# Two transformer blocks on one core: own PSUM tiles for the last two chunks of a product, the first two chunks side by side, the last residual first, the lambdas early

## The chip, the core and the metric

The kernel runs on one core of a Trainium2 chip. The core has TensorE for matrix products, VectorE and ScalarE for work on tiles, GpSimd (POOL) for small work, and SyncE (SP), whose queue issues nearly all transfers. They run side by side, each through its own list of instructions in order, and wait for one another by semaphores. The metric is the time of one execution in device microseconds.

## What is computed

Everything is float32, 256 positions of 1024 features, batch 1. The first block, once:

```python
proj = rmsnorm(h, g) @ w_in                    # q, k, v, u, y
attn = dilated_mixture_attention(rope(q), rope(k), v)
rec  = bidirectional_rglru(conv(u), ...) * gelu(y)
h = h + concat([attn, rec]) @ w_out
h = h + memory_cross_attention(rmsnorm(h), rmsnorm(mem), w_cq, w_ck, w_cv, w_co)
h = h + square(relu(rmsnorm(h) @ w_mlp_in)) @ w_mlp_out      # 1024 -> 4096 -> 1024
x = rmsnorm(h)
```

and the second, twice (two layers):

```python
z = rmsnorm(x) @ w_in_2                        # inputs of four mixers and 4 x 1024 gates
merged = sum(sigmoid(gate[n]) * (mixer[n](z) @ w_branch[n]) for n in range(4))
x = x + merged @ w_out_2                       # mixers: latent attention, Fourier, differential
h2 = rmsnorm(x)                                #   attention (with a lambda), gated recurrence
x = x + (silu(h2 @ w_gate) * (h2 @ w_up)) @ w_down           # 1024 -> 2 x 2816 -> 1024
```

The lambda of the differential attention is `exp(sum(lq1*lk1)) - exp(sum(lq2*lk2))` and a constant; the recurrence has lower bounds for its forget gates. Both come from small parameters alone.

## The kernel before

Features lie on the 128 partitions, positions along the rows, so the 1024 features are eight slices `k` of 128. A product is computed in **chunks** of 128 output features; a chunk needs all K slices of its input (K = 8, for `w_mlp_out` 32, for `w_down` 22).

**Weights.** All weights come as one stream of blocks, 128 x 1024 elements of 512 KB each, `w`, in the order in which `plan` lists them: kind "F" goes through all K slices of one chunk before the next, kind "T" through all listed columns of one slice before the next slice. Five blocks are in flight at most. ScalarE rounds a block to the type fp32r, `whi` (L353), VectorE computes the remainder `wlo` (L354), and inputs are treated alike: `xx`, `hd`, `fw` have a high and a low part. `lin` multiplies hi by hi, hi by lo and lo by hi, three matmuls of 256 columns (L378 to L380, in `mm3`). `lin_w` does the same with two: L575 takes high and low part of the input side by side, 512 columns, L576 adds the low weights, 256 columns.

**PSUM and consumers.** `lin` puts a pair of chunks into one tile `pl` of 2 KB a partition. `lin_w` puts a pair into one tile `pw` of 4 KB, each chunk in its own half; there are two such tiles. What is done with a finished pair (`consume`) is noted in `self.pend` and emitted by `flush` after the next pair's first chunks. With `fine=True` the last two chunks are not taken as a pair: each is consumed as soon as it is there.

**The seam.** The consumer of the products that end in the residual stream is `residual` (L1126 to L1138). For `lin_w`, ScalarE copies one part to `rs` (L588), VectorE adds the other (L589), multiplies by the norm's factor (L1133) and adds to `h` (L1134). Then `prep` makes the slice `xx` of the next product's input: its high part on ScalarE (L385), its low part on VectorE (L389), and squares for the next norm. So each product's first chunk needs, with its last slice `k` = 7, the residual of the last chunk of the product before.

**Order.** The program is written stage by stage; a scheduler then orders the instructions of each engine by its own estimates of time and by priorities (`high_priority(n)` moves work ahead by n). So an engine may do work of the next stage between two chunks of this one. `mixers` run beside the products by such priorities.

**Small parameters.** `hgrn_bounds` (L1235) makes the bounds of the forget gates; `diff_lambdas` (L1253) loads `lq`, multiplies (`lqp`, L1262), sums (`lqs`), exponentiates on GpSimd (`lqe`). Both are called at the start of the second block (L1779, L1780). The tables of a layer (`tabs`, `dt`, L1291 to L1303) and its small weights (`sw`, L1282) are loaded before each layer. At the start of the kernel, SyncE also loads `mem` (L747) and swaps halves of `qe` for the rotary embedding through `sw<-qe` (L698).

Of the kernel before, what the change touches and what calls it, by code (L numbers as in the profile page):

```python
# [9 lines left out]
F32 = mybir.dt.float32  # L10
# [9 lines left out]
T = 256  # L20
D = 1024
KD = D // 128
# [6 lines left out]
NW = 5  # L29
SB = 8  # L30
WARM = 36
G4, H2 = 16, 12
A0, A1 = 2, 4
X0, X1 = 1, 3
D0, D1 = 2, 4
M0, M1 = 1, 2
HA, HR, HM, HN = 200, 100, 100, 400

# [28 lines left out]
def plan():  # L67

    p = []
    r = np.arange  # L70

    def f(key, idx, cols):
        p.append((key, idx, cols, "F"))

    def t(key, idx, cols):
        p.append((key, idx, cols, "T"))

    t("w_in", (0,), 1536 + r(512))
    f("w_in", (0,), r(512))
    f("w_in", (0,), 512 + r(512))  # L80
    t("w_in", (0,), 1024 + r(512))
    f("w_in", (0,), 2048 + r(512))
    f("w_ck", (0,), r(512))
    f("w_out", (0,), r(1024))
    f("w_cq", (0,), r(512))
    t("w_cv", (0,), r(512))
    f("w_co", (0,), r(1024))
    f("w_mlp_in", (0,), r(4096))
    f("w_mlp_out", (0,), r(1024))
    for l in range(LAYERS):  # L90
        f("w_in_2", (l,), _forget_cols())
        t("w_in_2", (l,), _cols("fnet"))
        for n in ("hq", "hg", "dq", "dk", "c_kv"):
            f("w_in_2", (l,), _cols(n))
        f("w_in_2", (l,), _krope_cols())
        f("w_in_2", (l,), _cols("c_q"))
        t("w_in_2", (l,), np.concatenate([_cols("hi"), _cols("dv")]))
        for n in BRANCHES:
            w = 1024 if n != BRANCHES[-1] else 256
            for o in range(0, 1024, w):  # L100
                f("w_in_2", (l,), _cols("gate")[n * 1024 + o:n * 1024 + o + w])
                f("w_branch_2", (l, n), o + r(w))
        f("w_out_2", (l,), r(1024))
        f("w_gate_up_2", (l,), np.concatenate(
            [np.concatenate([j * 128 + r(128), FF2 + j * 128 + r(128)]) for j in range(FF2 // 128)]))
        f("w_down_2", (l,), r(1024))
    return p
# [372 lines left out]
def run(gen):  # L480
    for _ in gen:
        pass
# [26 lines left out]
class Body(Kern):  # L509
# [24 lines left out]
        for f, a in p:  # L534
            f(*a)

    def lin(self, key, idx, M, act, consume, K=KD, fine=False, half=False, m0=0):


        self.segment(key, idx, M * 128, "F")  # L540
        for m in range(0, M, 2):
            n = min(2, M - m)
            ps = self.psl("pl").rearrange("p (c t) -> p c t", c=2)
            one = fine and m + 2 >= M
            for c in range(n):
                for k in range(K):
                    wh, wl = self.wtile()
                    xh, xl = act(k)
                    self.mm3(ps[:, c, :], wh, wl, xh, xl, k == 0, k == K - 1)
                self.tick()  # L550
                if c == n - 1 or one:
                    self.flush()
                if one:
                    consume(m0 + m + c, ps[:, c:c + 1], 1)
                if half and c < n - 1:
                    yield
            if n == 1:
                self.tick()
            if not one:
                self.pend.append((consume, (m0 + m, ps[:, :n], n)))  # L560
            yield

    def lin_w(self, key, idx, M, act, consume, K=KD, fine=False):


        self.segment(key, idx, M * 128, "F")
        mm = self.nc.tensor.matmul
        for m in range(0, M, 2):
            ps = self.pw.tile([128, 2, 2, T], F32, name="pw", tag="pw")
            one = fine and m + 2 >= M  # L570
            for c in range(2):
                for k in range(K):
                    wh, wl = self.wtile()
                    x = act(k)
                    mm(ps[:, c], wh, x, start=k == 0, stop=False, skip_group_check=True)  # L575
                    mm(ps[:, c, 0], wl, x[:, 0], start=False, stop=k == K - 1, skip_group_check=True)  # L576
                self.tick()
                if c == 1 or one:
                    self.flush()
                if one:  # L580
                    consume(m + c, ps[:, c:c + 1], 1)
            if not one:
                self.pend.append((consume, (m, ps, 2)))
            yield
# [300 lines left out]
    def act(self, xh, xl):  # L885
        return lambda k: (xh[:, k], xl[:, k])
# [24 lines left out]
    def block1(self):  # L911
# [235 lines left out]
        def c_cq(k, ps, n):  # L1147
            V.tensor_tensor(cq[:, k:k + n], ps, self.bT(r2["b"], n), op=OP.mult)

        run(self.lin("w_cq", (0,), 4, xact, c_cq))  # L1150
        ch, cl = self.g4("ch", F32R), self.g4("cl", F32R)

        def cross():
# [25 lines left out]
        self.flush()  # L1179
        r3 = self.norm_later(n3, "n3")  # L1180


        hid = [self.g4(f"hd{i}", F32R, [128, 2, 2, T]) for i in range(16)]

# [6 lines left out]
        run(self.lin_w("w_mlp_in", (0,), 32, lambda k: self.xx[:, k], c_mlp))  # L1191
        self.flush()
        b3 = r3["b"]
        V.tensor_tensor(b3, b3, b3, op=OP.mult)
# [80 lines left out]
    def layer(self, l, rx, nxt):  # L1275
# [385 lines left out]
        def c_merge(n, m):  # L1661
# [4 lines left out]
            def f(k, ps, c):  # L1666
# [7 lines left out]
                if n == BRANCHES[-1]:  # L1674
# [4 lines left out]
        items = [self.lin(k2, L, 4, x, c_forget), self.lin_t(k2, L, 256, x, c_fx), ("start", mixers[1]), self.lin(k2, L, 2, x, c_hq), ("start", mixers[3]),  # L1679
                 self.lin(k2, L, 2, x, c_hg), self.lin(k2, L, 2, x, scaled(dqe)), self.lin(k2, L, 2, x, scaled(dke)),  # L1680
                 ("start", mixers[2]),
                 self.lin(k2, L, 1, x, c_kv), self.lin(k2, L, 1, x, c_kr), self.lin(k2, L, 3, x, scaled(cq)),
# [2 lines left out]
        for n in BRANCHES:  # L1685
# [4 lines left out]
            for m in range(0, 8, M):  # L1690
# [7 lines left out]
        self.flush()  # L1698
        n6 = Norm(self)
        run(self.lin("w_out_2", L, 8, lambda k: (mh[k // 4][:, k % 4], ml[k // 4][:, k % 4]),  # L1700
                     self.residual(n6, self.G(f"ln_ffn{l}")), fine=True))
        self.flush()
        r6 = self.norm_later(n6, "n6")

# [8 lines left out]
            f = fw[k // 4][:, k // 2 % 2]  # L1713
            self.split(f[:, 0], f[:, 1], t[:, 1])

        run(self.lin_w("w_gate_up_2", L, 44, lambda k: self.xx[:, k], c_glu))
# [89 lines left out]
```

## Time and profile before

| | |
|---|---|
| median of 3 runs | 1310.23 us |
| lowest, highest | 1309.72, 2054.62 us |
| the profiled execution | 1312.75 us, of which its span is 1311.0 |
| mean granted clock of TensorE | 0.986 |
| busy: TensorE, its weight loads | 1269.3 us (97%), 1153.5 us (88%) |
| busy: VectorE, ScalarE, GpSimd | 919.6 us (70%), 721.9 us (55%), 85.0 us (6%) |
| read from memory | 208.37 MB, 160 GB/s over the span |

The span runs from the first to the last instruction. Busy time of an engine is the time in which it worked on instructions; matmuls overlap, and one that follows another starts before the other's end. In a timeline the number in square brackets is the idle time of the engine just before the instruction, and the arrow names what ended it. The granted clock is a share of TensorE's full speed: 1.00 is 2.4 GHz, 0.50 is 1.2 GHz.

### The profile page before, as it was taken

How to read it: one execution, taken by the hardware profiler on the slowest of the kernel's cores; microseconds unless marked ns; L12 is line 12 of the kernel's file. 1: busy time of each engine (PE TensorE's matmuls, PEld its weight loads, DVE VectorE, ACT ScalarE, POOL GpSimd, SP SyncE). 2: the span in 40 equal slices, each digit the busy share in tenths (PEclk: the TensorE clock that was granted, in tenths of full speed). 3: DMA queues.
4: the chain of work that ended last, by engine and by line, in shares of the span. 5: the costliest groups of instructions: out<-in, count | busy, mean ns of one | idle time of the engine just before them, and what ended most of it. 6: DMA issues, size and time to landing. Idle time of an engine off the chain costs nothing.

```text
span 1311.0 us, 21638 instructions
## 1 busy us (share of the span) xinstructions
PE 1269.3 (97%) x8514; PEld 1153.5 (88%) x8514; DVE 919.6 (70%) x1396; ACT 721.9 (55%) x1132; POOL 85.0 (6%) x105
## 2 busy tenths in 40 slices
PE   8989989999989999999999999999999999999998
PEld 8876978888879998899988887899989899888887
DVE  5986648775557985667767775669866677777754
ACT  5777556554446456544555553464574545655542
POOL 8010000000001300100000000003001000000000
PEclk9889999999999999999999999999998999999999
DMA  7642435555564452245555565554522355555562
GB/s 262 202 130 79 147 110 193 189 188 187 191 209 156 157 181 81 97 147 188 179 179 193 187 206 208 167 165 147 191 96 85 126 177 179 184 188 190 191 190 68
DMA packets 68741, 216.07 MB, mean 165 GB/s; under 512 B 10392, under 2 KB 16280, under 8 KB 68640
## 3 DMA queue, kind: packets, MB, share of 16 engines
q1 hardware_dynamic: 68592, 214.66, 50.1%
q8 instruction: 67, 1.10, 0.3%
q14 instruction: 34, 0.28, 0.1%
q0 software_dynamic: 48, 0.03, 0.0%
HBM read 208.37 MB, written 1.05 MB: 160 GB/s over the span
## 4 chain that ended last, share of the span: by engine, by line
PE 85%; DVE 5%; ACT 4%; POOL 2%; issue 2%; DMA 2%; SPq 0%; DVEq 0%; ACTq 0%; POOLq 0%
PE pw L575 27%; PE pw L576 14%; PE pl L379 11%; PE pl L378 11%; PE pl L380 11%; PE ph L1388 2%; DVE wlo L354 2%; ACT whi L353 1%; PE pl L620 1%; PE pl L619 1%; PE pl L621 1%; POOL rt L808 1%; ACT p L669 1%; PE pq L1541 1%; PE pod L1491 1%
## 5 line engine op out<-in xcount | busy, mean ns | idle before, releaser
L353 ACT ACTIVATE whi<-w 128x1024 fp32r<-128x1024 f32 (+1 forms) x386 | 403.9, 1050 | 463.3 <-issue 154.9
L354 DVE TENSOR_TENSOR wlo<-w,whi 128x1024 fp32r<-128x1024 f32 (+1 forms) x386 | 467.2, 1212 | 251.6 <-ACT whi L353 250.5
L575 PE MATMUL pw<-xx,whi 128*128 128x512 f32 x960 | 334.3, 392 | 0.3 <-DVE xx L389 0.3
L576 PE MATMUL pw<-xx,wlo 128*128 128x256 f32 x960 | 269.5, 281 | 0.1
L378 PE MATMUL pl<-xx,whi 128*128 128x256 f32 x912 | 262.0, 288 | 7.7 <-ACT xx L385 4.0
L380 PE MATMUL pl<-xx,wlo 128*128 128x256 f32 x912 | 263.8, 290 | 3.5 <-DVE wlo L354 3.5
L379 PE MATMUL pl<-xx,whi 128*128 128x256 f32 x912 | 262.4, 288 | 0.0
L575 PEld LDWEIGHTS pw<-xx,whi 128*128 128x128 f32 x960 | 179.7, 187 | 40.2 <-DVE xx L389 1.0
L378 PEld LDWEIGHTS pl<-xx,whi 128*128 128x128 f32 x912 | 176.8, 194 | 10.2 <-ACT xx L385 4.4
L380 PEld LDWEIGHTS pl<-xx,wlo 128*128 128x128 f32 x912 | 176.8, 194 | 7.4 <-DVE wlo L354 4.3
L576 PEld LDWEIGHTS pw<-xx,wlo 128*128 128x128 f32 x960 | 181.4, 189 | 0.4 <-DVE wlo L354 0.4
L379 PEld LDWEIGHTS pl<-xx,whi 128*128 128x128 f32 x912 | 176.8, 194 | 0.6 <-DVE xx L389 0.2
L575 PE MATMUL pw<-fw,whi 128*128 128x512 f32 x352 | 125.9, 401 | 2.6 <-DVE fw L387 1.7
L576 PE MATMUL pw<-fw,wlo 128*128 128x256 f32 x352 | 99.7, 283 | 0.8 <-DVE wlo L354 0.8
L575 PE MATMUL pw<-hd,whi 128*128 128x512 f32 x256 | 90.4, 397 | 2.7 <-DVE rs L589 2.7
L575 PEld LDWEIGHTS pw<-fw,whi 128*128 128x128 f32 x352 | 66.9, 190 | 19.4 <-DVE fw L387 2.0
L576 PE MATMUL pw<-hd,wlo 128*128 128x256 f32 x256 | 72.2, 282 | 0.0
L576 PEld LDWEIGHTS pw<-fw,wlo 128*128 128x128 f32 x352 | 67.3, 191 | 1.4 <-DVE wlo L354 1.4
L575 PEld LDWEIGHTS pw<-hd,whi 128*128 128x128 f32 x256 | 48.6, 190 | 13.8 <-DVE rs L589 3.0
L576 PEld LDWEIGHTS pw<-hd,wlo 128*128 128x128 f32 x256 | 49.1, 192 | 0.0
L378 PE MATMUL pl<-oh,whi 128*128 128x256 f32 x128 | 36.8, 291 | 0.7 <-ACT oh L385 0.7
L379 PE MATMUL pl<-ol,whi 128*128 128x256 f32 x128 | 36.6, 287 | 0.6 <-DVE ol L387 0.6
(429 smaller groups left out, 1997.3 us busy)
## 6 DMA issues: line engine op xcount, KB each, us to landing
w<-in_W_dram SPq DMA_DIRECT2D x378, 512.0 KB, 3.4
w<-in_W_dram SPq DMA_DIRECT2D x8, 256.0 KB, 4.7
sw<-in_S_dram SPq DMA_DIRECT2D x4, 512.0 KB, 6.2
h<-in_xT_dram SPq DMA_DIRECT2D x8, 128.0 KB, 4.8
mem<-in_memT_dram SPq DMA_DIRECT2D x2, 512.0 KB, 5.5
sw<-qe SPq DMA_DIRECT2D x16, 64.0 KB, 3.5
dt<-in_C_dram SPq DMA_DIRECT2D x4, 256.0 KB, 7.5
dqs<-dhi SPq DMA_DIRECT2D x16, 64.0 KB, 3.8
```

What stands on the lines that cost most here:

```text
L353: self.nc.scalar.activation(hi, w, AF.Copy)
L354: self.nc.vector.tensor_tensor(lo, w, hi.bitcast(F32), op=OP.subtract)
L378: mm(out, wh, xh, start=first, stop=False, skip_group_check=shared)
L379: mm(out, wh, xl, start=False, stop=False, skip_group_check=shared)
L380: mm(out, wl, xh, start=False, stop=last, skip_group_check=shared)
L575: mm(ps[:, c], wh, x, start=k == 0, stop=False, skip_group_check=True)
L576: mm(ps[:, c, 0], wl, x[:, 0], start=False, stop=k == K - 1, skip_group_check=True)
L619: mm(o, xh[:, s], wh, start=(k == 0), stop=False)
L620: mm(o, xh[:, s], wl, start=False, stop=False)
L621: mm(o, xl[:, s], wh, start=False, stop=(k == K - 1))
L669: nc.scalar.activation(p[:, q], src[:, q], AF.Exp, bias=nm[:, q:q + 1], scale=scale if number else scale[:, q:q + 1], accum_out=den[:, q:q ...
L1388: nc.tensor.matmul(ps[:, k], hk[:, 2 * hp + k // 2, s], qz[:, 2 * hp + k // 2, s], start=True, stop=True)
```

## The change

1. With `fine=True`, each of the last two chunks gets a PSUM tile of its own, in `lin` and in `lin_w`.
2. With the new `side=True`, the first two chunks of a product are computed side by side over the slices: slice 0 for both, slice 1 for both, and so on. Their weights come in that order in the stream (kind "T" for the first 256 columns). It is set for `w_cq`, `w_mlp_in`, the forget columns that begin `w_in_2`, `w_out_2` and `w_gate_up_2`.
3. The consumers of the last two chunks are emitted at high priority (`HF` = 400).
4. `hgrn_bounds` and `diff_lambdas` are called before `w_mlp_in` and no longer at the start of the second block.
5. In `lin`, with `half=True`, noted consumers are also flushed after the first chunk of a pair.
6. The buffers of the tag `h2` are 10 instead of 12.

```diff
-G4, H2 = 16, 12
+G4, H2 = 16, 10
...
-HA, HR, HM, HN = 200, 100, 100, 400
+HA, HR, HM, HN, HF = 200, 100, 100, 400, 400
...
+    def tf(key, idx, cols):
+        t(key, idx, cols[:256])
+        f(key, idx, cols[256:])
...
-    f("w_cq", (0,), r(512))
+    tf("w_cq", (0,), r(512))
...
-    f("w_mlp_in", (0,), r(4096))
+    tf("w_mlp_in", (0,), r(4096))
...
-        f("w_in_2", (l,), _forget_cols())
+        tf("w_in_2", (l,), _forget_cols())
...
-        f("w_out_2", (l,), r(1024))
-        f("w_gate_up_2", (l,), np.concatenate(
+        tf("w_out_2", (l,), r(1024))
+        tf("w_gate_up_2", (l,), np.concatenate(
...
+    def order(self, key, idx, M, K, m, side):
+        if m == 0:
+            if side:
+                self.segment(key, idx, 256, "T")
+            else:
+                self.segment(key, idx, M * 128, "F")
+        elif m == 2 and side:
+            self.segment(key, idx, (M - 2) * 128, "F")
+        n = min(2, M - m)
+        if side and m == 0:
+            return [(c, k) for k in range(K) for c in range(n)]
+        return [(c, k) for c in range(n) for k in range(K)]
...
     # in lin
-            ps = self.psl("pl").rearrange("p (c t) -> p c t", c=2)
             one = fine and m + 2 >= M
-            for c in range(n):
-                for k in range(K):
-                    wh, wl = self.wtile()
-                    xh, xl = act(k)
-                    self.mm3(ps[:, c, :], wh, wl, xh, xl, k == 0, k == K - 1)
+            ps = [self.psl("pl").rearrange("p (c t) -> p c t", c=2) for _ in range(n if one else 1)]
+            for i, (c, k) in enumerate(self.order(key, idx, M, K, m, side)):
+                o = ps[c][:, 0] if one else ps[0][:, c]
+                wh, wl = self.wtile()
+                xh, xl = act(k)
+                both = side and m == 0
+                self.mm3(o, wh, wl, xh, xl, k == 0 and not (both and c), k == K - 1, both)
+                if (i + 1) % K:
+                    continue
+                c = i // K
                 self.tick()
-                if c == n - 1 or one:
+                if c == n - 1 or one or half:
                     self.flush()
                 if one:
-                    consume(m0 + m + c, ps[:, c:c + 1], 1)
+                    with self.tc.high_priority(HF):
+                        consume(m0 + m + c, ps[c][:, :1], 1)
...
     # in lin_w
             ps = self.pw.tile([128, 2, 2, T], F32, name="pw", tag="pw")
-            one = fine and m + 2 >= M
-            for c in range(2):
-                for k in range(K):
-                    wh, wl = self.wtile()
-                    x = act(k)
-                    mm(ps[:, c], wh, x, start=k == 0, stop=False, skip_group_check=True)
-                    mm(ps[:, c, 0], wl, x[:, 0], start=False, stop=k == K - 1, skip_group_check=True)
+            po = [ps[:, 0], ps[:, 1]]
+            if one:
+                po[1] = self.pw.tile([128, 2, 2, T], F32, name="pw", tag="pw")[:, 0]
+            for i, (c, k) in enumerate(self.order(key, idx, M, K, m, side)):
+                wh, wl = self.wtile()
+                x = act(k)
+                mm(po[c], wh, x, start=k == 0, stop=False, skip_group_check=True)
+                mm(po[c][:, 0], wl, x[:, 0], start=False, stop=k == K - 1, skip_group_check=True)
...
                 if one:
-                    consume(m + c, ps[:, c:c + 1], 1)
+                    with self.tc.high_priority(HF):
+                        consume(m + c, po[c].rearrange("p (o a) t -> p o a t", o=1), 1)
...
         r3 = self.norm_later(n3, "n3")
+        self.hgrn_bounds()
+        self.diff_lambdas()
...
         rx = self.between(n4, n5)
-        self.hgrn_bounds()
-        self.diff_lambdas()
```

**TensorE at the end of `w_mlp_out`**, from the seventh to the eighth output chunk (`pw` is the tile in PSUM with its number, `hd0` to `hd15` the hidden slices, two in each). Before:

```order
L575 MATMUL pw_3660<-hd15_2251,whi_3685 128x512
L576 MATMUL pw_3660<-hd15_2251,wlo_3686 128x256
L575 MATMUL pw_3660<-hd0_2236,whi_3707 128x512
L576 MATMUL pw_3660<-hd0_2236,wlo_3708 128x256
L575 MATMUL pw_3660<-hd0_2236,whi_3707 128x512
```

With the change:

```order
L601 MATMUL pw_3685<-hd15_2276,whi_3711 128x512
L602 MATMUL pw_3685<-hd15_2276,wlo_3712 128x256
L601 MATMUL pw_3686<-hd0_2261,whi_3733 128x512
L602 MATMUL pw_3686<-hd0_2261,wlo_3734 128x256
L601 MATMUL pw_3686<-hd0_2261,whi_3733 128x512
```

Before, the eighth chunk goes into the tile of the seventh, 3660; now it goes into another one, 3686.

**VectorE at the end of `w_mlp_out`**, from the next layer's tables to the last slice of the next product's input (`rs` and `h` with 256 columns are the residual of the last chunk). Before:

```order
L1302 TENSOR_SCALAR dt<-dt,pt 128x256 x2
L354 TENSOR_TENSOR wlo<-w,whi 128x1024
L1303 TENSOR_SCALAR dt<-dt,pt 128x256 x2
L354 TENSOR_TENSOR wlo<-w,whi 128x1024 x2
L589 TENSOR_TENSOR rs<-pw,rs 128x256
L1133 TENSOR_TENSOR rs<-rs,n3b 128x256
L1262 TENSOR_TENSOR lqp<-lq 128x64 x2
L1134 TENSOR_TENSOR h<-h,rs 128x256
L1264 TENSOR_REDUCE lqs<-lqp 128x4
L1305 TENSOR_SCALAR gc<-pt 128x1
L1306 TENSOR_SCALAR gc<-pt 128x1
L389 SCALAR_TENSOR_TENSOR xx<-h,misc,xx 128x256
```

With the change:

```order
L1332 TENSOR_SCALAR tabs<-tabs,pt 128x256 x2
L1333 TENSOR_SCALAR tabs<-tabs,pt 128x256
L358 TENSOR_TENSOR wlo<-w,whi 128x1024
L1335 TENSOR_SCALAR dt<-dt,pt 128x256 x2
L1336 TENSOR_SCALAR dt<-dt,pt 128x256 x2
L358 TENSOR_TENSOR wlo<-w,whi 128x1024
L619 TENSOR_TENSOR rs<-pw,rs 128x256
L1163 TENSOR_TENSOR rs<-rs,n3b 128x256
L1164 TENSOR_TENSOR h<-h,rs 128x256
L358 TENSOR_TENSOR wlo<-w,whi 128x1024
L393 SCALAR_TENSOR_TENSOR xx<-h,misc,xx 128x256
```

`lqp`, `lqs` and `gc` have left this place, and a `wlo` now stands between `h` and `xx`; the tables and some `wlo` stand ahead of `rs`, as they did. Behind the last chunk TensorE now has 58 matmuls of the next product ahead of the first that needs the last `xx`, where it had 42.

**SyncE near the start of the kernel**, from the weight blocks that follow the first tables to the first rope swap (`gb` are gate matrices). Before:

```order
L339 DMA w<-in_W_dram 128x1024 x4
L747 DMA mem_519<-in_memT_dram 128x1024
L747 DMA mem_520<-in_memT_dram 128x1024
L339 DMA w<-in_W_dram 128x1024
L741 DMA gb_462<-in_gw_dram 64x8x64 x2
L741 DMA gb_463<-in_gw_dram 64x8x64
L339 DMA w<-in_W_dram 128x1024
L741 DMA gb_463<-in_gw_dram 64x8x64
L339 DMA w<-in_W_dram 128x1024 x3
L698 DMA sw<-qe 32x512 x8
```

With the change:

```order
L343 DMA w<-in_W_dram 128x1024 x5
L771 DMA gb_462<-in_gw_dram 64x8x64 x2
L771 DMA gb_463<-in_gw_dram 64x8x64 x2
L343 DMA w<-in_W_dram 128x1024 x3
L777 DMA mem_521<-in_memT_dram 128x1024
L777 DMA mem_522<-in_memT_dram 128x1024
L343 DMA w<-in_W_dram 128x1024
L728 DMA sw<-qe 32x512 x4
L343 DMA w<-in_W_dram 128x1024
```

The two transfers of `mem` stood behind four weight blocks and ahead of the gate matrices; now they stand behind eight blocks and the gate matrices, one weight block ahead of the first `sw<-qe`.

## Rows read from the trace of the kernel before

**Rows 1.** The page's first part: busy time, share of the span, instructions.

```profile
PE 1269.3 (97%) x8514; PEld 1153.5 (88%) x8514; DVE 919.6 (70%) x1396; ACT 721.9 (55%) x1132; POOL 85.0 (6%) x105
```

**Rows 2.** Waits of TensorE: us in total, times, longest.

```profile
PE pl L378 <- ACT xx L385: 4.0, 2, 2.7
PE pw L575 <- DVE rs L589: 3.6, 2, 2.7
```

**Rows 3.** TensorE's timeline: start, us, line, operation [idle before, releaser].

```profile
81.31 0.47 PE L415 MATMUL mbp<-ct,mr 128*128 128x128 f32 x1 [3.53 <-POOL mr L397]
...
371.21 0.79 PE L575 MATMUL pw<-hd,whi 128*128 128x512 f32 x1 [2.67 <-DVE rs L589]
...
388.68 0.28 PE L379 MATMUL pl<-xx,whi 128*128 128x256 f32 x1
388.80 0.28 PE L380 MATMUL pl<-xx,wlo 128*128 128x256 f32 x1
391.79 0.80 PE L378 MATMUL pl<-xx,whi 128*128 128x256 f32 x2 [2.70 <-ACT xx L385]
...
637.63 0.39 PE L379 MATMUL pl<-mgl,whi 128*128 128x256 f32 x1 [0.22 <-DVE mgl L389]
...
661.46 0.50 PE L575 MATMUL pw<-xx,whi 128*128 128x512 f32 x1 [0.15 <-DVE xx L389]
...
838.55 0.39 PE L378 MATMUL pl<-xx,whi 128*128 128x256 f32 x1 [0.38 <-ACT whi L353]
...
839.81 0.39 PE L380 MATMUL pl<-xx,wlo 128*128 128x256 f32 x1 [0.76 <-DVE wlo L354]
...
853.90 0.51 PE L378 MATMUL pl<-xx,whi 128*128 128x256 f32 x2 [1.25 <-ACT xx L385]
...
1298.44 0.50 PE L575 MATMUL pw<-fw,whi 128*128 128x512 f32 x1 [0.93 <-DVE rs L589]
```

**Rows 4.** TensorE by stretch: us, busy (matmuls), granted clock, DMA share, GB/s.

```profile
81.30:84.30 3.00, 2.99 (x12) 0.50 0.33 104
...
371.20:374.40 3.20, 3.19 (x10) 0.50 0.59 188
375.00:378.20 3.20, 3.20 (x20) 1.00 0.91 295
...
391.80:394.90 3.10, 3.10 (x14) 0.50 0.00 0
```

**Rows 5.** VectorE's timeline, columns as in Rows 3.

```profile
51.74 0.68 DVE L964 TENSOR_TENSOR sw<-sw,rope 128x512 f32<-128x512 f32 x1
...
205.28 0.47 DVE L389 SCALAR_TENSOR_TENSOR xx<-h,pt,xx 128x256 fp32r<-128x256 f32 x1
...
370.74 0.42 DVE L589 TENSOR_TENSOR rs<-pw,rs 128x256 f32<-128x256 f32 x1
...
380.64 0.61 DVE L1299 TENSOR_SCALAR tabs<-tabs,pt 128x256 f32<-128x256 f32 x2 [2.62 <-DMA tabs<-in_C_dram]
...
390.49 0.36 DVE L1262 TENSOR_TENSOR lqp<-lq 128x64 f32<-128x64 f32 x2 [3.35 <-DMA lq<-in_lq_dram]
390.77 0.42 DVE L1134 TENSOR_TENSOR h<-h,rs 128x256 f32<-128x256 f32 x1
...
391.76 0.48 DVE L389 SCALAR_TENSOR_TENSOR xx<-h,misc,xx 128x256 fp32r<-128x256 f32 x1 [0.26 <-ACT xx L385]
```

**Rows 6.** The page's costliest groups, the split on VectorE: busy, mean ns, idle before.

```profile
L354 DVE TENSOR_TENSOR wlo<-w,whi 128x1024 fp32r<-128x1024 f32 (+1 forms) x386 | 467.2, 1212 | 251.6 <-ACT whi L353 250.5
```

**Rows 7.** SyncE's timeline, columns as in Rows 3.

```profile
40.16 1.87 SPq L698 DMA_DIRECT2D sw<-qe  x3
...
200.40 0.33 SPq L339 DMA_DIRECT2D w<-in_W_dram  x1
```

**Rows 8.** The page's DMA issues: times, KB each, us to landing.

```profile
mem<-in_memT_dram SPq DMA_DIRECT2D x2, 512.0 KB, 5.5
```

**Rows 9.** The tile `qe`, sixteen swap transfers: us from issue to landing.

```profile
DMA to landing us min/median/max: 1.9/3.5/6.2
```

More of the change, by code (lines that the diff above doesn't have):

```diff
@@ L535, in flush, with lin @@
             f(*a)
-    def lin(self, key, idx, M, act, consume, K=KD, fine=False, half=False, m0=0):
-        self.segment(key, idx, M * 128, "F")
+    def order(self, key, idx, M, K, m, side):
[10 more added lines that the diff above has]
+        return [(c, k) for c in range(n) for k in range(K)]
+    def lin(self, key, idx, M, act, consume, K=KD, fine=False, half=False, m0=0, side=False):
         for m in range(0, M, 2):
             n = min(2, M - m)
-            ps = self.psl("pl").rearrange("p (c t) -> p c t", c=2)
             one = fine and m + 2 >= M
-            for c in range(n):
-                for k in range(K):
-                    wh, wl = self.wtile()
-                    xh, xl = act(k)
-                    self.mm3(ps[:, c, :], wh, wl, xh, xl, k == 0, k == K - 1)
+            ps = [self.psl("pl").rearrange("p (c t) -> p c t", c=2) for _ in range(n if one else 1)]
[8 more added lines that the diff above has]
+                c = i // K
                 self.tick()
-                if c == n - 1 or one:
+                if c == n - 1 or one or half:
                     self.flush()
                 if one:
-                    consume(m0 + m + c, ps[:, c:c + 1], 1)
+                    with self.tc.high_priority(HF):
+                        consume(m0 + m + c, ps[c][:, :1], 1)
                 if half and c < n - 1:
@@ L559, in lin, with lin_w @@
             if not one:
-                self.pend.append((consume, (m0 + m, ps[:, :n], n)))
+                self.pend.append((consume, (m0 + m, ps[0][:, :n], n)))
             yield
-    def lin_w(self, key, idx, M, act, consume, K=KD, fine=False):
-        self.segment(key, idx, M * 128, "F")
+    def lin_w(self, key, idx, M, act, consume, K=KD, fine=False, side=False):
         mm = self.nc.tensor.matmul
         for m in range(0, M, 2):
+            one = fine and m + 2 >= M
             ps = self.pw.tile([128, 2, 2, T], F32, name="pw", tag="pw")
-            one = fine and m + 2 >= M
-            for c in range(2):
-                for k in range(K):
-                    wh, wl = self.wtile()
-                    x = act(k)
-                    mm(ps[:, c], wh, x, start=k == 0, stop=False, skip_group_check=True)
-                    mm(ps[:, c, 0], wl, x[:, 0], start=False, stop=k == K - 1, skip_group_check=True)
+            po = [ps[:, 0], ps[:, 1]]
[6 more added lines that the diff above has]
+                mm(po[c][:, 0], wl, x[:, 0], start=False, stop=k == K - 1, skip_group_check=True)
+                if (i + 1) % K:
+                    continue
+                c = i // K
                 self.tick()
@@ L1148, in c_cq @@
             V.tensor_tensor(cq[:, k:k + n], ps, self.bT(r2["b"], n), op=OP.mult)
-        run(self.lin("w_cq", (0,), 4, xact, c_cq))
+        run(self.lin("w_cq", (0,), 4, xact, c_cq, side=True))
         ch, cl = self.g4("ch", F32R), self.g4("cl", F32R)
@@ L1189, in c_mlp @@
             self.split(hid[k // 2][:, :, 0], hid[k // 2][:, :, 1], t2)
-        run(self.lin_w("w_mlp_in", (0,), 32, lambda k: self.xx[:, k], c_mlp))
+        run(self.lin_w("w_mlp_in", (0,), 32, lambda k: self.xx[:, k], c_mlp, side=True))
         self.flush()
@@ L1678, in layer @@
         mixers = {n: urgent(self.tc, m, HM) for n, m in ((3, hgrn()), (2, diff()), (0, mla()), (1, fnet()))}
-        items = [self.lin(k2, L, 4, x, c_forget), self.lin_t(k2, L, 256, x, c_fx), ("start", mixers[1]), self.lin(k2, L, 2, x, c_hq), ("start", mixers[3]),
+        items = [self.lin(k2, L, 4, x, c_forget, side=True), self.lin_t(k2, L, 256, x, c_fx), ("start", mixers[1]), self.lin(k2, L, 2, x, c_hq), ("start", mixers[3]),
                  self.lin(k2, L, 2, x, c_hg), self.lin(k2, L, 2, x, scaled(dqe)), self.lin(k2, L, 2, x, scaled(dke)),
@@ L1700, in layer @@
         run(self.lin("w_out_2", L, 8, lambda k: (mh[k // 4][:, k % 4], ml[k // 4][:, k % 4]),
-                     self.residual(n6, self.G(f"ln_ffn{l}")), fine=True))
+                     self.residual(n6, self.G(f"ln_ffn{l}")), fine=True, side=True))
         self.flush()
@@ L1714, in c_glu @@
             self.split(f[:, 0], f[:, 1], t[:, 1])
-        run(self.lin_w("w_gate_up_2", L, 44, lambda k: self.xx[:, k], c_glu))
+        run(self.lin_w("w_gate_up_2", L, 44, lambda k: self.xx[:, k], c_glu, side=True))
         self.flush()
```

## The prediction

> **What bounds the kernel now.** The page's first part comes first: TensorE is busy 97% of the span [rows 1], so the kernel can only become faster by fewer matmuls (the change has as many) or by closing the places in which TensorE stands. Idle is only 1311.0 - 1269.3, about 42 us. The view of TensorE's waits says for whom it stands: 4.0 us for ScalarE's `xx`, 3.6 us for VectorE's `rs` [rows 2]. TensorE's timeline then places each wait [rows 3]. The 3.6 us for `rs` are two waits before the last output chunk of a product: 2.67 at 371.21 (`w_mlp_out`) and 0.93 at 1298.44 (the second `w_down`). The 4.0 us for `xx` are the first matmul that reads the last eighth of the next stage's input: 2.70 at 391.79 and 1.25 at 853.90. So the stage to look at is the seam: a product's last chunks, the residual sum, the preparation of `xx`, the next product's first chunks.
>
> The windows on TensorE give the hidden part of the price. After each of the two long waits the granted clock is 0.50, the level of 1.2 GHz: 3.20 us at 371.20 with 10 matmuls where 20 fit at 375.00, and 3.10 us at 391.80 again at 0.50 [rows 4]. Half the work of about 3.2 us is lost, 1.6 us each. I count such a stretch behind waits of this length alone, not behind the 0.93 and 1.25.
>
> **Part A, own tile.** In `lin_w` both chunks of a pair share one tile, so the last chunk's first matmul waits until the `rs` of the chunk before has read it. VectorE took up that `rs` at 370.74 [rows 5] and TensorE went on at 371.21 [rows 3]. After the change it writes a tile of its own, whose former user is the pair before. That pair was due a whole chunk earlier, 64 matmuls at 20 in 3.20 us [rows 4] or some 10 us, so the estimate for the wait is zero. What is removed: 2.67 + 1.6 of half clock at 371, and 0.93 at 1298: 5.2 us. What could eat it: TensorE now wants the next split weights 2.7 us sooner. At 375.00 it takes them at full speed and without a gap [rows 4], so I take nothing. The rule that speaks against this part is the Trainium skill's, "PSUM — Partial Sum Buffer", section "PSUM bank collisions raise a hardware error": engines are to be kept apart by bank, so a reader in another bank stops no matmul. The two halves of the tile are two banks; by that rule there would be no wait to remove, and the sum would be 5.2 us smaller. The rows show the wait, with VectorE's `rs` as its releaser, so here the program's dependency goes by the tile, and the trace decides.
>
> **Part B, the lambdas early.** At the end of `w_mlp_out`, VectorE finished its part of `rs` at 387.1 (390.49 - 3.35) and then stood 3.35 us in `lqp` for a small transfer of `lq`. `h` came behind it at 390.77 and the last `xx` at 391.76 [rows 5]. TensorE had run through the 42 matmuls that didn't need it and waited 2.70 us [rows 3]. With `lqp` gone, `h` starts at 387.1 and `xx` 1.0 us later, before the cover runs out. At 0.12 us from matmul to matmul (388.68, 388.80 [rows 3]) 42 last 5.0 us, and the change raises them to 58, 7.0 us. A `wlo` of 1.2 us [rows 6] now stands between `h` and `xx`; 58 matmuls carry that too. Removed: 2.70 + 1.6 = 4.3 us.
>
> `lqp` is not gone but moved: it stands now before the last `xx` of the seam from `w_co` to `w_mlp_in`, which came at 205.28 [rows 5]. By SyncE's order its transfer goes out right behind the weight block that went out at 200.40 [rows 7]; if it takes 5.5 us as the transfers of `mem` did [rows 8], it lands at about 206, near the time at which `xx` was due. Bounds: nothing, and a hold as long as the one seen, 3.35 [rows 5]. Since landing and need nearly meet, and TensorE's cover there grows by some 0.8 us, I expect a wait between 0 and 0.9 and take 0.4. The rest of the lambdas, and the bounds of the forget gates, are some ten short VectorE operations beside the cross-attention's tail, where TensorE already waits in places: 0 to 0.7, I take 0.3.
>
> **Part C, side by side and the last residual first.** At the first layer's `w_down`, 18 matmuls of the next layer were slipped in before the last chunk. They waited 0.38 and 0.76 for their weights, and left only 24 behind the last chunk, 2.9 us, so that `xx` was 1.25 late [rows 3]. The change puts none ahead and 58 behind (7.0 us); `xx` needed 2.9 + 1.25 = 4.2. Removed: 0.38 + 0.76 + 1.25 = 2.4 us. Side by side also doubles the matmuls per eighth of the input wherever a stage starts: the waits of 0.22 at 637.63 (for `mgl`) and 0.15 at 661.46 (for `xx`) [rows 3] have a twin each in the second layer, at 1100.64 and 1124.47; 0.74 us in all. The interleaving itself adds no matmul and no weight load. The order of the weights in the stream changes, not their number or size; the pool of residual buffers shrinks from 12 to 10, and by the order at most about 7 are in use. I cost both at nothing.
>
> **The start.** The order of SyncE's queue shows a move that the diff doesn't: the two 512 KB transfers of `mem` now go out after eight weight blocks and the gate tables, and ahead of the rope swap's transfers. A transfer of `mem` takes 5.5 us to land [rows 8]. The swap's first transfers were issued from 40.16 to 42.0 [rows 7] and took at most 6.2 us [rows 9], so they were there by 48.2; VectorE first reads a swapped tile at 51.74 [rows 5], a slack of 3.5 us at least. With `mem` ahead I estimate that they land about 4 us later, so this comes out about even: 0, with bounds of 7 us gained (the GpSimd wait of 3.53 at 81.31 [rows 3] and the stretch at half clock behind it [rows 4], some 3 us, if the order around it becomes kinder) and 5 us lost.
>
> **Sum.** 5.2 + 4.3 + 2.4 + 0.7 = 12.6; less 0.4 and 0.3: about 12 us. The profiled execution took 1312.75 us (1311.0 of span and 1.75 around it), 2.5 above the median of the runs shown, 1310.23. In its terms the result is 1300.7, as a median **1298**.
>
> **The rivals.** *The gains are eaten again.* The last residual is put first, but in the order of VectorE the tables of the next layer (`tabs`, `dt`) and two `wlo` still stand ahead of it. `tabs` came at 380.64, held by its transfer [rows 5], 9.4 us after the last chunk's first matmul. Behind it stand seven table operations of 0.3 us each and two `wlo` of 1.2 [rows 5, 6], 4.5 us. In all that is 14 us, against about 11 for the chunk at full clock (64 matmuls); with the gate opening about a microsecond earlier at full clock, `rs` starts 2 to 3 us behind the chunk. Then come twice `rs` and `h`, 0.4 each, the `wlo` and `xx`, 3.3: 5.3 to 6.3 of the 7.0 that the cover lasts. If the transfer lands 1 to 2 us later than this, TensorE waits again and B's half-clock stretch comes back: up to 4.3; with 0.9 more for `lqp` and its own stretch, 6.8. Then 5 to 8 us are left: 1302 to 1306, and up to 1309 if a third seam is hit. For it: the margin is thin. Against it: the transfer is released by the last chunk's first matmuls, which now run at full clock, so it should be earlier.
>
> *The start gains too.* The order around 81 us has `mbp` 22 rows later on TensorE, which gives GpSimd's `mr` more time. If its 3.53 and the slow stretch of 3 go as well: 1298 - 6.5 = 1291, and with a little less idle before it, 1287 to 1291.
>
> *Slower than before.* VectorE stands at the first multiplication with a swapped tile, because `mem` lies ahead of it in the queue; `wlo` stands behind it, so TensorE runs dry and its clock falls to 1.2 GHz, as it did after the waits of 2.7 and 3.5 us [rows 3, 4]. Slack is about 4 us. For a loss beyond the 12 us won, the hold must be about 9 us (9 idle and some 3 of half clock), that is, the tile must land later than about 61. Two landings of `mem`, 5.5 us each and one after the other, put it at 48 + 11 = 59 only if nothing overlaps, which I hold unlikely. It would give 1313 to 1322.
>
> *The change doesn't do what it says*: the scheduler orders the work by its own estimates and gives each seam back. The order speaks against it: own tile, the place of `lqp` and the 58 matmuls are all there. About 1307 to 1311.
>
> **How the numbers follow.** Forecast (1292 to 1302): 0.58. Gains eaten (1302 to 1309): 0.22. The start gains too (1287 to 1292): 0.12. Slower (1313 to 1322): 0.05. No effect: 0.03. The range reaches from the lower end of the start's gain to the upper end of the eaten gains: 1288 to 1309, which leaves out the slower case, most of no effect and the rims. Two per cent, 26 us, is about what a measurement of this kernel can tell from no change. Faster than 1284 needs every case's gain at once and more: 0.03. Slower than 1336 needs a hold at the start twice as long as the slower rival's: 0.02. Within: 0.95.
>
> **What the changed profile would show.** A: no wait for `rs` before the last chunk of `w_mlp_out` and of the second `w_down`, and full clock there. B: no `lq` among VectorE's waits at the seam to the next block, and `xx` before its 58 matmuls end. C: no wait for `whi`, `wlo` or `xx` around the first `w_down`. Wrong: a wait of over 1 us for `xx` behind `tabs`, a hold in `lqp` near 205, or a wait for `sw` on VectorE near 52. If the stalls are gone and the time is not, something else than TensorE's idle time was lost, and its busy time or clock must show it.

## The result, and the profile after

The changed kernel took 1289.35 us (median of 4 runs, 1287.15 to 1292.48), the kernel before 1309.97; the ratio is 0.984, with a 95% interval of 0.982 to 0.986. That is 20.6 us less, where 12 were predicted: inside the stated range (1288 to 1309), beyond the band of the forecast (1292 to 1302), and in that of the rival by which the start gains too (1287 to 1292). One run of the kernel before took 2054.62 us; the ratio leaves it out.

The page's first part, of the changed kernel:

```profile
span 1285.3 us, 21650 instructions
...
PE 1257.4 (98%) x8514; PEld 1146.8 (89%) x8514; DVE 918.1 (71%) x1396; ACT 720.3 (56%) x1132; POOL 85.2 (7%) x105
```

Its view of TensorE's waits, us in total, times and longest:

```profile
PE po L1118 <- ACT pts L720: 3.2, 3, 1.7
PE pl L382 <- ACT whi L357: 2.9, 2, 2.5
PE pl L384 <- DVE wlo L358: 2.1, 1, 2.1
PE sd L1506 <- ACT p L699: 1.6, 2, 1.1
```

The two rows that led before, the waits for `xx` and for `rs` [rows 2], are gone. What leads now lies in the attention, whose row for `pts` was 1.5 us in 2 waits before, and at 32 to 34 us, where both kernels wait. In the windows of [rows 4], the clock is full:

```profile
81.30:84.30 3.00, 3.00 (x28) 1.00 0.37 128
371.20:374.40 3.20, 3.20 (x26) 1.00 1.04 403
391.80:394.90 3.10, 3.10 (x28) 1.00 0.00 0
```

These windows hold other work than before, since the stages come earlier (the last chunk of `w_mlp_out` starts at 361.37), but the mean granted clock is 1.00 over the whole stretch from 40 to 511 us. The same TensorE work needs less busy time too (1257.4 against 1269.3 us [rows 1]), mostly because a matmul at half clock counts as busy for twice as long [rows 4]: up to the last matmul this trace has 13.7 us at half clock, that of before 34.1. Not all of that is the change: two more traces of the changed kernel (experiment 4) have 23.9 and 27.3.

The last residual of `w_mlp_out`, on VectorE (the row of work that [rows 5] shows from `tabs` to `xx`):

```profile
370.19 0.62 DVE L1332 TENSOR_SCALAR tabs<-tabs,pt 128x256 f32<-128x256 f32 x2 [0.82 <-DMA tabs<-in_C_dram]
...
374.83 0.42 DVE L619 TENSOR_TENSOR rs<-pw,rs 128x256 f32<-128x256 f32 x1
375.29 0.43 DVE L1163 TENSOR_TENSOR rs<-rs,n3b 128x256 f32<-128x256 f32 x1
375.75 0.42 DVE L1164 TENSOR_TENSOR h<-h,rs 128x256 f32<-128x256 f32 x1
376.50 1.23 DVE L358 TENSOR_TENSOR wlo<-w,whi 128x1024 fp32r<-128x1024 f32 x1 [0.33 <-ACT whi L357]
377.65 0.48 DVE L393 SCALAR_TENSOR_TENSOR xx<-h,misc,xx 128x256 fp32r<-128x256 f32 x1
```

The chunk's last matmul started at 372.35; `rs` came 2.5 us behind it and `xx` ended at 378.13, 5.8 behind it. The 58 matmuls last 7.0. TensorE didn't stand there.

**Where the time went.** From the traces: the time from the last matmul of one product to the last of the next, in us. The first stage ends at `mbp`.

| up to the last matmul of | before | after | after, second trace | own tile alone | without own tile |
|---|---|---|---|---|---|
| (`mbp`) | 81.31 | 79.66 | 80.56 | 82.07 | 79.83 |
| `w_out` | 72.39 | 65.99 | 65.99 | 68.66 | 69.93 |
| `w_co` | 48.62 | 49.72 | 49.73 | 49.01 | 47.33 |
| `w_mlp_in` | 88.30 | 88.23 | 88.22 | 89.40 | 87.68 |
| `w_mlp_out` | 93.17 | 88.75 | 88.75 | 88.75 | 94.64 |
| `w_out_2`, first layer | 274.66 | 267.78 | 269.38 | 270.47 | 270.63 |
| `w_gate_up_2` | 121.04 | 122.96 | 122.96 | 124.92 | 120.18 |
| `w_down_2` | 70.00 | 63.40 | 64.74 | 64.06 | 67.38 |
| `w_out_2`, second layer | 271.97 | 268.24 | 269.95 | 269.92 | 269.70 |
| `w_gate_up_2` | 120.86 | 122.95 | 122.96 | 124.92 | 122.22 |
| `w_down_2` | 63.74 | 62.68 | 62.68 | 61.78 | 63.99 |
| sum to the last matmul | 1306.06 | 1280.37 | 1285.91 | 1293.95 | 1293.53 |

A gate stage that grows by 2 us only takes work that the stage ahead of it gave up (matmuls that were slipped in before), so the two are read together. Four places carry the gain: the first two stages together 8.1 us; `w_mlp_out` 4.4; the first layer's `w_out_2` with its gate stage 5.0 (3.4 in the second trace), where the wait at 391 stood; and the first `w_down_2` 6.6 (5.3). Of the last, some 2.2 us are only work that moved to the next stage (18 matmuls of 0.12), and 1.7 are a stretch at half clock behind a wait for `fw`, which no term of the prediction names and which none of the three traces of the changed kernel has. The two traces of one and the same program differ by 5.5 us, so the pair of profiles (25.7 apart) flatters the change; the comparison of runs is the measure.

### The profile page after: what moved, and what is told of

It reads as the page before. It is cut to its first block, busy times and chain, and to the rows that moved or that the text cites. A ratio compares the mean times of both kernels' runs of the same rounds, so it can differ in the third digit from the quotient of the medians.

```text
span 1285.3 us, 21650 instructions
## 1 busy us (share of the span) xinstructions
PE 1257.4 (98%) x8514; PEld 1146.8 (89%) x8514; DVE 918.1 (71%) x1396; ACT 720.3 (56%) x1132; POOL 85.2 (7%) x105
## 4 chain that ended last, share of the span: by engine, by line
PE 89%; DVE 3%; ACT 2%; POOL 2%; DMA 1%; issue 1%; SPq 1%; DVEq 0%; ACTq 0%; POOLq 0%
PE pw L601 28%; PE pw L602 14%; PE pl L383 11%; PE pl L382 11%; PE pl L384 11%; PE ph L1421 2%; PE pl L649 1%; PE pl L650 1%; PE pl L651 1%; POOL rt L838 1%; PE ptp L717 1%; PE pq L1574 1%; ACT p L699 1%; SPq L1488 1%; PE pod L1524 1%
```

## The experiments

All were run against the kernel before on the same chip, and the ratios are to it. The first four do one part alone, or nothing.

**1. The own tile alone.** The hunks of the diff on `ps` and `po`, without side by side, priority and the rest:

```diff
+            po = [ps[:, 0], ps[:, 1]]
+            if one:
+                po[1] = self.pw.tile([128, 2, 2, T], F32, name="pw", tag="pw")[:, 0]
...
-                    mm(ps[:, c], wh, x, start=k == 0, stop=False, skip_group_check=True)
+                    mm(po[c], wh, x, start=k == 0, stop=False, skip_group_check=True)
```

> The kernel before with one part of the change: an own PSUM tile for each of the last two chunks. Theory (the wait is by the tile): no wait of TensorE for rs before the last chunk of w_mlp_out and of the second w_down, and no half clock at 371; that is 2.67 + 1.6 + 0.93 = 5.2 us. By the order of TensorE this part alone also ends the 18 matmuls that were slipped in before the last chunk of the first w_down, so some of the 2.4 us of that seam go too: 5 to 7.5 us in all, about 1303 to 1305 where the kernel before takes 1310. The hold in lqp at the end of w_mlp_out stays, with its 2.70 and its half clock. Rival (the last chunk waits for VectorE anyway, by the weights or by rs itself): the wait moves behind the last chunk and the time is that of before within 1.5 us.

Measured: 1298.38 us, ratio 0.991 (0.990 to 0.993), some 11 us. Both waits for `rs` are gone, and so are all three waits at the first `w_down_2`. The hold in `lqp` stayed, with this on TensorE:

```profile
385.55 0.38 PE L379 MATMUL pl<-xx,whi 128*128 128x256 f32 x1 [2.12 <-DVE xx L389]
```

On VectorE `lqp` stands behind `h` in this kernel, and the last `xx` waited for it all the same. The own tile is more than half of the gain, more than I expected of it: the rows of Part A and of Part C at the first `w_down_2` make 7.6 us (5.2 and 2.4), and no experiment says where the other 3 come from.

**2. The lambdas early, alone.**

```diff
+        self.hgrn_bounds()
+        self.diff_lambdas()
...
         rx = self.between(n4, n5)
-        self.hgrn_bounds()
-        self.diff_lambdas()
```

> The kernel before with the calls of the bounds and lambdas put ahead of w_mlp_in, nothing else. Theory: the 2.70 us for xx at 391.79 and the half clock behind it go, 4.3 us, and the new place costs at most 0.9: 1306 to 1307. Rival 1 (the hold in lqp only moves): a wait of VectorE for lq of 1 us or more near 205, TensorE waits there, about 1309 to 1310. Rival 2 (the last xx is late for another reason, tabs or rs): TensorE still waits over 1 us near 391, about 1308.

Measured: 1306.77 us, ratio 0.9986 (0.9974 to 0.9997), about 2 us, as the theory had it. But rival 1 holds in part: the wait at 391 is gone, and a new one stands at the place to which `lqp` was moved. VectorE held for `lq`:

```profile
204.87 0.36 DVE L1265 TENSOR_TENSOR lqp<-lq 128x64 f32<-128x64 f32 x2 [0.90 <-DMA lq<-in_lq_dram]
```

and TensorE stood behind it, for the last `xx`:

```profile
207.01 0.50 PE L575 MATMUL pw<-xx,whi 128*128 128x512 f32 x1 [1.13 <-DVE xx L389]
```

**3. The flush of half pairs, alone.** One line:

```diff
-                if c == n - 1 or one:
+                if c == n - 1 or one or half:
                     self.flush()
```

> The kernel before with one line of the change: the flush after the first chunk of a pair where half is set. By the order this alone moves mem behind eight weight blocks and the product mbp 22 matmuls later. Theory (it is this line that brought the gain at the start): the wait of 3.53 us for GpSimd's mr at 81.31 falls under 1 us and the half clock from 80.9 to 87.7 goes (3.4 us), some 1.2 of waits at 72 to 74 go, and the attention behind it loses about 2: 5 to 7 us less than before, 1303 to 1305. Rival (the gain at the start came from other parts or differs from run to run): no difference, 1310.

Measured: 1302.50 us, ratio 0.9950 (0.9935 to 0.9965), about 6.6 us. Its `mbp`:

```profile
79.48 0.32 PE L415 MATMUL mbp<-ct,mr 128*128 128x128 f32 x1 [0.25 <-POOL mr L397]
```

The wait was 3.53 before [rows 3], and the granted clock stays at full speed from 40 to 364 us, where it fell at 81 before. The first two stages take 147.86 us in this trace, 5.8 less than before. This line, which the title of the change doesn't name (it is part 5), is the gain at the start.

The same trace says something of the wait at 391 too. The lambdas and VectorE's order there are as before, yet VectorE held for `lq` 0.98 us and not 3.35, and TensorE stood 0.33 for `xx` and not 2.70:

```profile
383.51 0.36 DVE L1262 TENSOR_TENSOR lqp<-lq 128x64 f32<-128x64 f32 x2 [0.98 <-DMA lq<-in_lq_dram]
```

`lq` landed 4.1 us after its issue, where it took 5.2 before. So the 2.70 of [rows 3] is not a fixed price of that order.

**4. The changed kernel again, twice**, for the spread.

> The changed kernel once more, for the spread from run to run and a second trace. Theory (its gain is waits that the program's order sets): the same waits to 0.2 us at the same places, 1287 to 1293. Rival (part of it is luck of one execution, above all the GpSimd result at 80 us, the tables' transfer at 773 and the half clock at 965): some of these waits or half-clock stretches come back in this trace, each worth 1.5 to 3.5 us.

> The changed kernel a third time, beside the three kernels that lack one part. Theory: 1287 to 1293, no wait for rs, mr or the last xx; the runs lie in two groups some 4 us apart, by the wait for fw near 775 and the stretches at half clock. Rival: one of the seams' waits shows in this trace.

Measured: 1291.57 us, ratio 0.986 (0.984 to 0.988), and 1291.54 us, 0.9855 (0.984 to 0.987). The waits for `rs` and the last `xx` show in none of the three traces; the one for `mr` is 0.2 to 0.5 us in each. What comes and goes is the wait for `fw`, here on TensorE in the first trace:

```profile
773.15 0.50 PE L601 MATMUL pw<-fw,whi 128*128 128x512 f32 x1 [0.45 <-DVE fw L391]
```

and in the second:

```profile
776.98 0.50 PE L601 MATMUL pw<-fw,whi 128*128 128x512 f32 x1 [1.80 <-DVE fw L391]
```

It is 1.47 in the third. Stretches at half clock of different length come and go as well, near 35, 510, 940 and 970 us, in the third trace also at 124. The rival was right in so far: some 1.4 us of the first trace's gain and part of its clock were luck.

The next four leave one part out of the changed kernel.

**5. Without the own tile.**

```diff
-            if one:
-                po[1] = self.pw.tile([128, 2, 2, T], F32, name="pw", tag="pw")[:, 0]
```

> The changed kernel without the own tile: the last two chunks share one tile again, all else stays. Theory (the own tile alone was worth 10.8 us and the parts add up): the waits for rs before the last chunk of w_mlp_out (2.7, with half clock) and of the second w_down (0.9) come back, and by the order 23 matmuls are slipped in again before the last chunk of the first w_down with their waits: 8 to 11 us more than the changed kernel, 1298 to 1301. Rival (side by side and priority cover the seams without it): under 5 us more.

Measured: 1301.67 us, ratio 0.994 (0.992 to 0.996), 10 to 11 us more than the changed kernel beside it (1291.54 us, 0.9855). All that the theory named came back, to within a hundredth:

```profile
365.38 0.79 PE L601 MATMUL pw<-hd,whi 128*128 128x512 f32 x1 [2.67 <-DVE rs L619]
...
826.11 0.39 PE L382 MATMUL pl<-xx,whi 128*128 128x256 f32 x1 [0.38 <-ACT whi L357]
...
1285.77 0.51 PE L601 MATMUL pw<-fw,whi 128*128 128x512 f32 x1 [0.93 <-DVE rs L619]
```

Side by side and priority are in this kernel, and don't cover it.

**6. Without the flush of half pairs** (the line of experiment 3 taken out).

> The changed kernel without the flush after the first chunk of a pair: the order at the start is that of the kernel before. Theory: the wait of 3.5 us for GpSimd's mr and its half clock come back, 5 to 7 us more than the changed kernel, 1295 to 1297; mr itself lasts 5.6 us again instead of 3.9. Rival (the other parts also moved the start): no wait of over 1 us there, 1290.

Measured: 1295.15 us, ratio 0.989 (0.987 to 0.991), some 4 us more than the changed kernel beside it (3.6 by the medians, 4.6 by the ratios), less than the 5 to 7 expected. `mbp` waits 3.54 us again:

```profile
82.50 0.32 PE L419 MATMUL mbp<-ct,mr 128*128 128x128 f32 x1 [3.54 <-POOL mr L401]
```

GpSimd's `mr` lasts 5.62 again.

**7. Without the early lambdas** (experiment 2 reversed).

> The changed kernel with the bounds and lambdas called at the start of the second block again. Theory 1 (58 matmuls of cover and 2.7 us less ahead don't hide a hold of 1 to 3.4 us in lqp): TensorE waits 1 to 2 us for xx behind w_mlp_out, with half clock in some runs: 1.5 to 4 us more, 1291 to 1294. Theory 2 (with the side by side the cover is long enough, and the early call brings nothing any more): no wait there over 0.3 us, 1289 to 1291.

Measured: 1288.67 us, ratio 0.984 (0.982 to 0.986), the same as the changed kernel. Theory 2 held in its number, but not for its reason alone. VectorE at that seam:

```profile
376.41 0.42 DVE L1164 TENSOR_TENSOR h<-h,rs 128x256 f32<-128x256 f32 x1
377.17 1.23 DVE L358 TENSOR_TENSOR wlo<-w,whi 128x1024 fp32r<-128x1024 f32 x1 [0.34 <-ACT whi L357]
378.32 0.35 DVE L1292 TENSOR_TENSOR lqp<-lq 128x64 f32<-128x64 f32 x2
```

`lqp` stands behind `h` now and no longer ahead of it, and VectorE doesn't wait for `lq`, which was issued 5.1 us earlier. The other parts had already put it out of the way. Which of them did isn't shown; the own tile by itself didn't (2.12 us in experiment 1).

**8. Without side by side.** `side=True` removed at all five calls, `tf` back to `f`.

> The changed kernel without the side by side: every product's first two chunks one after the other, the weights in the old order. Theory (the own tile, the lambdas and the flush carry the gain; side by side is a small cover): the waits for mgl of 0.22 come back twice, and the hold in lqp near 199 shows on TensorE as it did with the lambdas alone (1.1 us for xx at 207): 1 to 3 us more than the changed kernel, 1291 to 1294. Rival (the cover of 58 matmuls is what closes the seams): waits for xx of over 1 us at the seams behind w_mlp_out and the first w_down, with half clock, 5 us or more: 1295 and above.

Measured: 1291.62 us, ratio 0.988 (0.986 to 0.990): 0 to 4 us more than the changed kernel, not told apart from none by these intervals. The trace has the small waits that the theory named, 0.34 for `xx` at 199.85 and 0.22 for `mgl`, and none behind `w_mlp_out`. It is a small cover.

**The priority** has no run of its own: with `HF` = 0 the program is the same, instruction for instruction in the same order on all five queues. "Last residual first" moved nothing. The smaller pool (part 6) has no run either, so its share isn't known.

The last three try to get more.

**9. The tables ahead of the small weights.** In `layer`, the two `dma_start` of `sw` are put behind those of `tabs` and `dt`.

> The changed kernel with the tables of a layer (tabs, dt) loaded ahead of its two 512 KB pieces of small weights instead of behind them. Theory (the wait for fw at 773, 0.45 us in one trace of the changed kernel and 1.80 in the other, is VectorE held by the tables' transfer, which lies behind a megabyte): VectorE's wait for tabs goes at both places, TensorE's wait for fw too: 1 to 2.5 us less, and runs that differ less. Rival (the tables are gated by the same release as the small weights and land as late, or the small weights are now late for the mixers): no difference, within 1 us.

Measured: 1287.47 us, ratio 0.985 (0.982 to 0.988), no difference to be seen, and the runs lie wider apart (1286.5 to 1295.6). The trace is that of the slowest of the five. In it the wait for `tabs` is 0 at one place and 0.36 at the other, but at the second VectorE now stands 1.24 for `dt`, with a `wlo` behind it:

```profile
773.10 0.62 DVE L1335 TENSOR_SCALAR dt<-dt,pt 128x256 f32<-128x256 f32 x2 [1.24 <-DMA dt<-in_C_dram]
...
774.36 1.22 DVE L358 TENSOR_TENSOR wlo<-w,whi 128x1024 fp32r<-128x1024 f32 x1
```

TensorE waited for that `wlo`:

```profile
775.63 0.58 PE L602 MATMUL pw<-fw,wlo 128*128 128x256 f32 x1 [2.53 <-DVE wlo L358]
```

The theory isn't borne out: in this trace the hold went from one table to the next. Experiment 11, which has the same edit, shows TensorE 2.70 us behind the same `wlo`, with VectorE held 2.07 for `tabs`. Of the three runs below 1288 there is no trace.

**10. The sines of the rotary tables late.**

`r` is the result of the first norm; the other sine and the absolute value ahead of it are tied to `z` likewise.

```diff
+        nc.vector.tensor_scalar(z, r[:, 0:1], 0.0, None, op0=OP.mult)
...
-        nc.scalar.activation(self.rope_sc[:, 1], a, AF.Sin)
+        nc.scalar.activation(self.rope_sc[:, 1], a, AF.Sin, bias=z)
```

> The changed kernel with the sines of the rotary tables tied to the first norm's result: ScalarE and VectorE take them up some 5 us later and don't stand for GpSimd's chain from 22 to 30 us. The values are the same. Theory (both engines hold the weights' split there): TensorE's waits of 2.5 and 2.1 us at 32 to 34 and the half clock from 33 to 40 (3.4 us) go, 5 to 8 us less. Rival (TensorE then waits for the first norm, which is behind the same chain on GpSimd, or the rope tables are late for the first products at 51): the wait moves, gain under 2 us or a loss.

Measured: 1289.34 us, ratio 0.986 (0.984 to 0.988): nothing gained. The weights' waits at 32 to 34 are gone and the rival's wait stands there, since the norm is behind the same chain on GpSimd; `mbp` waits again too. On TensorE:

```profile
33.60 0.43 PE L419 MATMUL n1p<-ct,n1r 128*128 128x128 f32 x2 [4.50 <-POOL n1r L401]
...
80.66 0.47 PE L419 MATMUL mbp<-ct,mr 128*128 128x128 f32 x1 [4.04 <-POOL mr L401]
```

**11. Both.**

> The changed kernel with both: the tables ahead of the small weights and the sines tied to the first norm. Theory: the two are 700 us apart and add up: 6 to 10 us less than the changed kernel, 1280 to 1285. Rival: one of the two brings nothing (see there), 1286 to 1290.

Measured: 1291.99 us, ratio 0.987 (0.985 to 0.989): the rival, nothing gained. No version was clearly faster than the changed kernel.

## Why the prediction was right and where it was not

**Part A** (5.2 us): right in mechanism and size. `w_mlp_out` lost 4.42 us in every kernel with the own tile, where 2.67 + 1.6 was predicted, and in none without; the second `w_down_2` lost 1 to 2, with 0.93 predicted. By the rule of the Trainium skill's "PSUM — Partial Sum Buffer", section "PSUM bank collisions raise a hardware error", that was weighed against it there would have been no wait to remove. The own tile alone made 11 us, so here the dependency goes by the tile although its halves are two banks.

**Part C** (2.4 and 0.7): the size was right, the cause was not, so that hit is luck. I gave the end of the slipped-in matmuls to side by side and the priority. Experiment 1 has neither, and they are gone; experiment 5 has both, and they are back. It was the own tile. Of the 0.7, the waits for `mgl` come back without side by side, those of 0.15 for `xx` don't (the own tile alone removes them). Side by side also covers the last third of what Part B costs: the wait for `xx` behind `w_co` was 1.13 with the early lambdas alone, 0.34 without side by side, and is none in the changed kernel.

**Part B** (4.3, less 0.7): the wait was removed as predicted, but the early call isn't what removes it in this kernel. Alone it was worth 2 us, since its new place cost 1.13 us on TensorE where I had taken 0.4 and expected 0.9 at most; together with the rest, nothing. So the 4.3 us of this term are in the total, but the early call is not needed for them. The wait of before hung on a position in VectorE's queue, which the own tile shifts as well, and on when `lq` landed: with the old position it was 0.33 in experiment 3, with the new one 2.12 in experiment 1. Which of the parts close it together stays open.

**The start** (0, with 7 gained as the bound): the failing step. It was worth 6.6 us alone and some 4 in the changed kernel. I had read from the order that `mbp` moves 22 matmuls back and had the price of its wait, 3.53 and a stretch at half clock, and still let an estimated delay of the swap transfers cancel it. That delay is a wait of VectorE for the swap of 0.8 us at most, in some of the traces, and TensorE doesn't stand behind it. The rival by which the start gains got 0.12; by its row (a wait of 3.53, and now 22 more matmuls of 0.12, 2.6 us, ahead of it) it deserved most of the weight. What no row of before could say is that `mr` itself would end 1.74 us sooner (see the last section). And I never asked which line moves it: part 5 of the change has no cost of its own in the prediction.

**The sum.** 5.2 + 2.4 + 0.7 + 6.6 and the 2 of Part B are 17 us, against 18 to 21 measured. The parts alone (11 + 2 + 6.6) make 20, so they add up within the noise, but not part by part: left out of the changed kernel, the own tile costs 10 to 11, the early lambdas nothing, the flush some 4 and side by side 0 to 4. The prediction also held that 26 us is about what a measurement of this kernel can tell from no change; the intervals here are 0.1 to 0.3% either way, 1.5 to 3.5 us.

**The rivals.** The margin for "eaten again" was as thin as stated: in the three traces `rs` came 2.5, 3.4 and 2.9 us behind the chunk (2 to 3 predicted), the chain ended at 5.8, 6.3 and 5.8 of 7.0 (5.3 to 6.3 predicted), and TensorE never waited there. The slower case showed only as those 0.8 us of VectorE.

## What to carry to other kernels

Look for a wait on the reader of another part of the same tile: an own buffer for the last piece cost nothing that shows here, and it also frees the scheduler from filling the hole with work of the next stage. A change of several parts is to be costed line by line, the line that its title leaves out too, and where the order puts more work ahead of a waiting instruction, the price of that wait (idle and half clock) is the first estimate, not zero. Moving one hold out of an in-order queue can let the next one through: experiments 2 and 9 did just that.

## What the runs showed of the hardware

One GpSimd operation of one shape (`mr`, 128x2) lasted 5.62 us before, 3.88 in the changed kernel and 4.42 in experiment 10; the like operation `n1r` there took 0.71. In each of the traces `mr` ended some 0.64 us after the start of the first VectorE instruction behind it that reads one input from PSUM: before it was `sb`, in experiment 10 `yt`. VectorE before:

```profile
75.48 1.21 DVE L354 TENSOR_TENSOR wlo<-w,whi 128x1024 fp32r<-128x1024 f32 x1
76.61 0.68 DVE L965 TENSOR_TENSOR kr<-qe,sw 128x512 f32<-128x512 f32 x1
...
80.62 0.41 DVE L657 CUSTOM_DVE_ANT_0 sb<-sc,lnc 128x256 f32<-128x256 f32 x1
```

GpSimd before, whose `mr` ends at 81.25:

```profile
75.63 5.62 POOL L397 TENSOR_TENSOR mr<-v,misc 128x2 f32<-128x2 f32 x1 [39.14 <-DVE v L395]
```

VectorE in experiment 10:

```profile
79.97 0.68 DVE L1079 TENSOR_TENSOR yt<-pl,n1b 128x512 f32<-128x512 f32 x1
```

and GpSimd there, with the end of `mr` at 80.61:

```profile
76.19 4.42 POOL L401 TENSOR_TENSOR mr<-v,misc 128x2 f32<-128x2 f32 x1 [42.64 <-DVE v L399]
```

Until then VectorE ran, without a gap, instructions with two inputs from SBUF. The trace of before has eleven GpSimd operations of this shape: besides `mr`, five took 1.51 to 1.73 us, each begun 0.07 to 0.25 us behind the start of a `wlo`, and five took 0.69 or 0.70, none begun while a `wlo` ran. Two of them:

```profile
399.34 1.54 POOL L397 TENSOR_TENSOR n4r<-v,misc 128x2 f32<-128x2 f32 x1 [6.78 <-DVE v L395]
401.62 0.70 POOL L397 TENSOR_TENSOR n5r<-v,misc 128x2 f32<-128x2 f32 x1 [0.74 <-DVE v L395]
```

The Trainium skill, "SBUF — State Buffer", section "Who interferes with whom", says that a VectorE instruction with two SBUF inputs contends with a GpSimd instruction that reads SBUF, since its second input comes through a read interface that the two engines share, and that this is an exclusive lock; the traces agree. The 1.74 us by which `mr` got shorter are two such instructions, `kr` and `tr` (starts 0.60 and 1.13 us apart from the next), which the flush of half pairs put elsewhere. No experiment took the port away by itself, so this cause is read from the coincidence in all fourteen traces and from these eleven operations, not shown by an experiment.
